# A hybrid DeltaNet/mLSTM layer on one core: masks of later heads moved along the projections, a fourth place for the scan's scaled values, sign changes as three-operand instructions

## The chip, the cores and the metric

The kernel runs on one core of one Trainium2 chip. The metric is the device time of one execution in microseconds (us), as the median of several runs. The engines are named as in the profile: PE (TensorE, matmuls; PEld are its weight loads), DVE (VectorE), ACT (ScalarE), POOL (GpSimd) and SP (SyncE, which here only issues DMAs).

## The reference, cut to what matters

One layer over 512 latent tokens with a prefix of 256 context tokens, all in float32, D_MODEL 1024. Two token mixers read one input projection: a bidirectional gated DeltaNet with 8 heads (called GDN here) and a bidirectional mLSTM with 4 heads. Their outputs are merged by gates, projected, and a gated MLP with a 3x3 convolution follows.

```
    kb = k * beta[..., None]
    a_strict = jnp.einsum('bhnld,bhnsd->bhnls', kb, k) * decay
    rhs = jnp.concatenate([v * beta[..., None], kb * jnp.exp(gc)[..., None]], axis=-1)
    sol = lax.linalg.triangular_solve(a_strict, rhs, left_side=True, lower=True, unit_diagonal=True)
    u, w = sol[..., :dv], sol[..., dv:]
...
        attn = jnp.einsum('bhnld,bhnsd->bhnls', q, k) * decay
...
        v_new = u_n - jnp.einsum('bhld,bhde->bhle', w_n, s)
        s_next = s * gt_n[..., None, None] + jnp.einsum('bhld,bhle->bhde', kt_n, v_new)
        o = jnp.einsum('bhld,bhde->bhle', qd_n, s) + jnp.einsum('bhls,bhse->bhle', at_n, v_new)
```

`decay` is exp of a masked difference of cumulated log decays, one 128x128 tile per chunk of 128 tokens and direction in the kernel: six chunks (two of context, four latent) by two directions are 12 tiles per GDN head, and four latent chunks by two directions are 8 tiles per mLSTM head.

## The kernel before, in words

**Stages.** After loads, modulation and the first norm, `mixers` (L1212) runs the two mixers; the rest (branch projections and gates, output projection, second norm, MLP) follows and is not touched. In the mixers each GDN head goes through `gdn_prep` (L714), `inverses` (L819, 16x16 triangular inverses on POOL, through DRAM), `merges` (L855, 16 to 128 by matmuls), `gdn_scan` (L956) and `gdn_tail` (L1019); each mLSTM head through `ml_prep` (L1057), `ml_scan` (L1126) and `ml_tail` (L1169). The preparation of heads 0 and 1 comes first, with nothing else to run. Then there is one step per head, s = 0 to 11: the scan of head s is driven by `drive` (L1195), which between two pieces of the scan draws pieces of the preparation of a head two or three ahead (and of early gate projections, `gate_mm` L1308) and of side work: the tail of head s-1, the merges of head s+1, gates of the mLSTM, and `ada_late` (L286), in which POOL weighs blocks of the matrix w_ada and adds them up, and a small matmul (`ada_sum` L316, tile `pad`) sums over partitions.

**Order.** Every instruction stands in its engine's queue in the order that the framework's tile scheduler gives from its own simulation, with hints: `queue_after` says that one instruction comes behind another on its queue, and `follow` (L1190) does that for the current anchor of an engine (the scan's newest matmul, DVE or ACT instruction). An engine runs its queue strictly in that order.

**Preparation of a GDN head.** Projections of context and latent tokens (`pc_k`, `px_k`, `px_q`, `pc_v`, `px_v`, `px_z`) run in float32r halves (three matmuls L124, L125 for each of eight blocks). `conv_silu` (L646) takes each out of its PSUM bank with a short convolution (ACT L653, DVE L654, L655, ACT tanh L656, DVE L657). `decays` and `weights` (L699, L706) make the decay tiles `Eg`: a DMA brings a row to all partitions, the DVE adds a column and takes the minimum with a mask (L710, 12 instructions of 128x128), and ACT takes exp (L711). For head 0 and heads 3 to 7 the 12 masks are written right behind the context part of the k projection, for heads 1 and 2 behind the q projection. The scalars `sc` (four per chunk and direction, 128x6) are made by

```
            nc.vector.tensor_tensor(s[:, 0, :], rk2, self.colB[:, :, 2 + d, h], ALU.mult)
            nc.vector.tensor_scalar(s[:, 1, :], s[:, 0, :], -1.0, None, ALU.mult)
            nc.vector.tensor_tensor(s[:, 2, :], s[:, 0, :], self.colB[:, :, d, h], ALU.mult)
            nc.vector.tensor_scalar(s[:, 3, :], s[:, 2, :], -1.0, None, ALU.mult)
```

(L754 to L757). The products `pkk` (L770, k by k) are scaled by `sc` and `Eg` into `Bt` (which lies in the buffer `gx` for most heads; L773, 12 DVE instructions), which frees the PSUM banks that `pqk` (L778, k by q) takes next; `at` (L782) reads `pqk`. Then v is turned to token-major (`ps_tm_v`) and ACT scales it into `vt` (L799); q follows (`ps_tm_q`, L804).

**Scan step of a GDN head.** `p1` (L980) = k S; `X` (L984, DVE) from it; `p2` (L988) = T X; ACT makes two scaled copies of `p2` for each of two directions: `v3` (L996), which goes into the state by `p3` (L1000) and `S` (L1005, L1007, DVE), and `v2` (L1013), which goes into the output by `po` (L971). All of them have the tile name "v", with three places.

**mLSTM.** `ml_prep` makes its masks `Em` (8, at L710 too) in front of the two `mo` projections. In `ml_scan`, `mp` (L1151) is read by ACT into `mn` (L1155), `mpc` (L1143) updates the state, and ACT L1165 makes `mo`. In the last steps the gate projections' tanh (L1312) is an ACT instruction that reads PSUM into `x1`.

PSUM has eight banks: two for the scan, one for merges, one for `po`, two for preparation (`pkk`, `pqk`, `ps_tm_*`) and two for projections ("acc").

Of the kernel before, what the change touches and what calls it, by code (L numbers as in the profile page):

```python
# [9 lines left out]
F32 = mybir.dt.float32  # L10
F32R = mybir.dt.float32r
BF16 = mybir.dt.bfloat16
AF = mybir.ActivationFunctionType
# [53 lines left out]
class Kern:  # L67
# [218 lines left out]
    def ada_late(self):  # L286

        nc, eng = self.nc, self.nc.gpsimd

        def load(j):  # L290
            w = self.hold.tile([P, 4, P], F32, tag="aw", name=f"aw{j}", bufs=3)
            i, c0 = j % 2, 2048 + P * (j // 2)
            self.follow(nc.sync.dma_start(w, self.I["w_ada"][0][512 * i : 512 * i + 512, c0 : c0 + P].rearrange("(k p) c -> p k c", p=P)))
            return w

        w = load(0)
        for j in range(64):
            nxt = load(j + 1) if j < 63 else None
            g = eng.tensor_tensor(w, w, self.sc[:, 4 * (j % 2) : 4 * (j % 2) + 4, 0:1].broadcast_to([P, 4, P]), ALU.mult)  # L299
            self.follow(g)  # L300
            self.follow(g, "q")
            eng.tensor_tensor(w[:, 0:2, :], w[:, 0:2, :], w[:, 2:4, :], ALU.add)  # L302
            if j % 2 == 0:
                a = self.hold.tile([P, P], F32, tag="as", name=f"as{j}", bufs=6)
                eng.tensor_tensor(a, w[:, 0, :], w[:, 1, :], ALU.add)
            else:
                eng.tensor_tensor(w[:, 0, :], w[:, 0, :], w[:, 1, :], ALU.add)
                eng.tensor_tensor(a, a, w[:, 0, :], ALU.add)
                self.sums.append((j // 2, a))
            for _ in range(2):  # L310
                if self.pad is not None and len(self.sums) > 1:
                    self.ada_sum()
            w = nxt
            yield
# [383 lines left out]

    def decays(self, h):  # L699
        E = [self.decay_rows(d, h, list(range(NCH)), f"g{h}_{d}") for d in range(2)]  # L700
        for d in range(2):
            if not 0 < h < 3:
                self.weights(E[d], d, h, range(NCH))
        return E

    def weights(self, E, d, row, g):  # L706

        nc = self.nc
        for c in g:
            self.follow(nc.vector.scalar_tensor_tensor(E[:, c, :], E[:, c, :], self.colA[:, c, d, row : row + 1], self.mask[d], ALU.add, ALU.min), "v")  # L710
        nc.scalar.activation(E[:, g[0] : g[-1] + 1, :], E[:, g[0] : g[-1] + 1, :], AF.Exp)  # L711


    def gdn_prep(self, h):  # L714
# [5 lines left out]
        kT = hold.tile([P, NALL], F32, tag="kT", name=f"kT{h}", bufs=3)  # L720
        p = yield from self.acc(wk, f"k{h}", True)
        self.conv_silu(p, NCTX, 8 + h, kT[:, :NCTX], {"v": self.chain["u"]} if h == 0 else None)
        E = self.decays(h)
        wq = self.w_cols(w, P * h, f"wq{h}") if h else self.first["wq"]
        p = yield from self.acc(wk, f"k{h}", False)
        self.conv_silu(p, NT, 8 + h, kT[:, NCTX:], {"v": self.chain["u"]} if h == 0 else None)
        wv = self.w_cols(w, 2048 + P * h, f"wv{h}") if h else self.first["wv"]
        qT = hold.tile([P, NT], F32, tag="qT", name=f"qT{h}", bufs=3)
        p = yield from self.acc(wq, f"q{h}", False)
        self.conv_silu(p, NT, h, qT, self.chain if h == 0 else None)  # L730
        if 0 < h < 3:
            v, self.anchor["v"] = self.anchor.get("v"), self.last_v
            for d in range(2):
                self.weights(E[d], d, h, range(NCH))
            self.anchor["v"] = v

        kt = hold.tile([P, NCH, P], F32, tag="kt", name=f"kt{h}", bufs=3)
# [14 lines left out]
        for d in range(2):  # L752
            s = hold.tile([P, 4, NCH], F32, tag=f"sc{d}", name=f"sc{h}_{d}", bufs=3)
            nc.vector.tensor_tensor(s[:, 0, :], rk2, self.colB[:, :, 2 + d, h], ALU.mult)  # L754
            nc.vector.tensor_scalar(s[:, 1, :], s[:, 0, :], -1.0, None, ALU.mult)
            nc.vector.tensor_tensor(s[:, 2, :], s[:, 0, :], self.colB[:, :, d, h], ALU.mult)
            nc.vector.tensor_scalar(s[:, 3, :], s[:, 2, :], -1.0, None, ALU.mult)  # L757
            sc.append(s)

        i = (h + 1) % 3  # L760
# [195 lines left out]
    def gdn_scan(self, h):  # L956
# [16 lines left out]
        for st in range(NCH):  # L973
# [18 lines left out]
            if st < NCH - 1:  # L992
                v3 = []
                for d, c in enumerate(cs):
                    v3.append(tmp.tile([P, P], F32, tag="v", name=f"v3_{h}", bufs=3))
                    self.anchor["s"] = nc.scalar.activation(v3[d], p2[:, d, :], AF.Copy, scale=sc[d][:, 2 + j, c : c + 1])  # L996
                yield
                p3 = self.pt([P, 2, P], "sc", f"p3_{h}")
# [10 lines left out]
            if cs[0] >= CC:  # L1009
                for d, c in enumerate(cs):  # L1010
                    x = c - CC
                    v2 = tmp.tile([P, P], F32, tag="v", name=f"v2_{h}", bufs=3)
                    nc.scalar.activation(v2, p2[:, d, :], AF.Copy, scale=sc[d][:, j, c : c + 1])  # L1013
                    out(x, qs[d][:, x * P : x * P + P], S[d])
                    out(x, at[d][:, x, :], v2)
# [41 lines left out]
    def ml_prep(self, h):  # L1057
# [12 lines left out]
        qT = hold.tile([P, NT], F32, tag="qT", name=f"mqT{h}", bufs=3)  # L1070
        p = yield from self.acc(wq, f"mq{h}", False)
        nc.scalar.activation(qT, p, AF.Copy, scale=P ** -0.5)
        for d in range(2):
            self.weights(E[d], d, 8 + h, range(CC, NCH))
        og = []
        for b in range(2):
            p = yield from self.acc(wo, f"mo{h}", False)
            if b == 0:
                wo = self.w_cols(w, O_MO + MDV * h + P, f"mwo{h}_1")
            g = hold.tile([P, NT], F32, tag=("zs", "vt")[b], name=f"og{h}_{b}", bufs=3)  # L1080
# [227 lines left out]
    def gate_mm(self, i, n, out):  # L1308

        wg = self.w_cols(self.I["w_in"][0], (O_G1, O_G2)[i] + P * n, f"wg{i}_{n}")  # L1310
        p = yield from self.acc(wg, f"g{i}_{n}", False)
        self.nc.scalar.activation(out, p, AF.Tanh, scale=0.5)  # L1312
        return out

    def merge(self):
# [302 lines left out]
```

## Time and profile before

| | us |
|---|---|
| median of 3 runs | 1338.4 (1337.61 to 1341.63) |
| profiled execution, its own time | 1334.85 |
| its span | 1333.1 |
| PE busy | 1290.1 (97%) |
| DVE busy | 898.9 (67%) |
| ACT busy | 584.3 (44%) |
| POOL busy | 532.1 (40%) |

The profile's page gives busy time by engine, the span in 40 slices, the chain of work that ended last, and groups of instructions by line. The trace behind it answers what each engine waited for, one line's instructions, busy time of stretches, and the instructions of an engine in order of time. The page's share of the chain that ended last is PE 71%, DVE 8%, ACT 5%. The profiled execution is one more execution beside the three runs; it lies 3.55 us under their median.

### The profile page before, as it was taken

How to read it: one execution, taken by the hardware profiler on the slowest of the kernel's cores; microseconds unless marked ns; L12 is line 12 of the kernel's file. 1: busy time of each engine (PE TensorE's matmuls, PEld its weight loads, DVE VectorE, ACT ScalarE, POOL GpSimd, SP SyncE). 2: the span in 40 equal slices, each digit the busy share in tenths (PEclk: the TensorE clock that was granted, in tenths of full speed). 3: DMA queues.
4: the chain of work that ended last, by engine and by line, in shares of the span. 5: the costliest groups of instructions: out<-in, count | busy, mean ns of one | idle time of the engine just before them, and what ended most of it. 6: DMA issues, size and time to landing. Idle time of an engine off the chain costs nothing.

```text
span 1333.1 us, 24202 instructions
## 1 busy us (share of the span) xinstructions
PE 1290.1 (97%) x9454; PEld 1093.3 (82%) x9454; DVE 898.9 (67%) x1809; ACT 584.3 (44%) x1283; POOL 532.1 (40%) x679
## 2 busy tenths in 40 slices
PE   6997999999999999999999999999999999999997
PEld 5887778888888888989888878888788888888886
DVE  6877777957868665343737476445669789997943
ACT  5565564555655644333334345222343333333322
POOL 4312330123121238575857560000444555554543
PEclk9999999999999999999999999999999999999999
DMA  9534233332242335254443433436333333333221
GB/s 284 151 106 123 45 86 98 72 87 73 61 108 60 74 84 143 78 160 111 125 121 104 112 100 88 127 111 227 104 111 95 95 95 96 95 98 90 81 102 73
DMA packets 233248, 141.86 MB, mean 106 GB/s; under 512 B 32992, under 2 KB 215533, under 8 KB 233133
## 3 DMA queue, kind: packets, MB, share of 16 engines
q1 hardware_dynamic: 230973, 140.09, 37.4%
q8 instruction: 74, 1.21, 0.4%
q10 hardware_dynamic: 2160, 0.23, 0.1%
q14 instruction: 41, 0.34, 0.1%
HBM read 134.47 MB, written 5.82 MB: 105 GB/s over the span
## 4 chain that ended last, share of the span: by engine, by line
PE 71%; DVE 8%; ACT 5%; DMA 2%; issue 1%; POOL 1%; SPq 0%; POOLq 0%; ACTq 0%; DVEq 0%
PE pu L124 12%; PE pd L124 6%; PE pu L125 6%; PE py L124 4%; PE px_g L124 4%; PE pv L124 3%; PE pd L125 3%; PE py L125 2%; PE px_mo L124 2%; PE px_g L125 2%; PE po L971 2%; PE p L988 2%; PE pv L125 2%; PE px_z L124 1%; PE p L980 1%
## 5 line engine op out<-in xcount | busy, mean ns | idle before, releaser
L1588 DVE SCALAR_TENSOR_TENSOR y<-pu,fw,y 128x441 f32<-128x441 f32 (+2 forms) x352 | 229.6, 690 | 38.7 <-ACT y L1579 33.0
L299 POOL TENSOR_TENSOR aw<-aw,sc 128x512 f32<-128x512 f32 x64 | 69.7, 1092 | 51.9 <-DMA aw<-in_w_ada_dram 51.9
L148 POOL TENSOR_TENSOR rs<-pw_t,mhalf 128x1 f32<-128x1 f32 x14 | 7.9, 563 | 161.1 <-PE po L125 130.4
L148 POOL TENSOR_TENSOR kh<-pw_t,phalf 128x6 f32<-128x6 f32 x8 | 10.9, 1361 | 127.9 <-DVE pw_t L147 36.0
L302 POOL TENSOR_TENSOR aw<-aw 128x256 f32<-128x256 f32 x64 | 56.1, 880 | 2.9
L842 POOL MEMSET gx<- 96x16 f32 x8 | 1.0, 124 | 119.1 <-DMA gx<-scr 119.1
L1517 POOL TENSOR_TENSOR al<-y,ah 128x512 fp32r<-128x512 f32 x22 | 28.6, 1300 | 31.2 <-ACT ah L1516 31.2
L1342 DVE SCALAR_TENSOR_TENSOR x<-x,py 128x512 f32<-128x512 f32 x16 | 11.0, 688 | 41.9 <-PE py L125 41.9
L1147 DVE SCALAR_TENSOR_TENSOR C<-C,ge,mpc 128x257 f32<-128x257 f32 x32 | 15.3, 478 | 34.9 <-PE mpc L1143 34.8
L656 ACT ACTIVATE cv_t<-cv_y 128x512 f32<-128x512 f32 (+1 forms) x40 | 22.0, 549 | 38.1 <-DVE cv_y L655 36.7
L847 POOL TENSOR_TENSOR iv_t<-gx 96x14 f32<-96x14 f32 (+6 forms) x112 | 35.1, 313 | 8.0
L849 POOL TENSOR_TENSOR gx<-gx,iv_t 96x14 f32<-96x14 f32 (+6 forms) x112 | 33.7, 301 | 8.7
L1579 ACT ACTIVATE y<-pu,fw 128x512 f32<-128x512 f32 x44 | 29.9, 683 | 13.3 <-PE pu L125 10.4
L996 ACT ACTIVATE v<-p,sc 128x128 f32<-128x128 f32 x80 | 25.2, 365 | 21.6 <-PE p L988 21.5
L984 DVE SCALAR_TENSOR_TENSOR X<-p,colA,vt 128x128 f32<-128x128 f32 x80 | 24.0, 339 | 15.5 <-PE p L980 15.1
L1516 ACT CAST ah<-y 128x512 fp32r<-128x512 f32 x22 | 13.6, 619 | 46.7 <-DVE y L1515 46.7
L1515 DVE TENSOR_TENSOR y<-y,y 128x512 f32<-128x512 f32 x22 | 31.3, 1424 | 0.9
L710 DVE SCALAR_TENSOR_TENSOR Eg<-Eg,colA,mask 128x128 f32<-128x128 f32 x96 | 27.4, 356 | 3.3 <-DMA Eg<-gd 3.3
L1155 ACT ACTIVATE mn<-mp,colA 128x257 f32<-128x257 f32 x32 | 15.2, 474 | 32.5 <-PE mp L1151 30.6
L971 PE MATMUL po<-v,at 128*128 128x128 f32 x128 | 26.0, 285 | 2.1 <-ACT v L1013 2.1
L1013 ACT ACTIVATE v<-p,sc 128x128 f32<-128x128 f32 x64 | 22.9, 375 | 11.7 <-PE p L1000 8.8
L1007 DVE SCALAR_TENSOR_TENSOR S<-S,ge,p 128x128 f32<-128x128 f32 x64 | 19.1, 338 | 12.4 <-PE p L1000 12.1
(1222 smaller groups left out, 4571.4 us busy)
## 6 DMA issues: line engine op xcount, KB each, us to landing
aw<-in_w_ada_dram SPq DMA_DIRECT2D x64, 256.0 KB
uw<-in_w_ada_dram SPq DMA_DIRECT2D x16, 512.0 KB
Eg<-gd SPq DMA_DIRECT2D x16, 384.0 KB
qs<-gd SPq DMA_DIRECT2D x16, 256.0 KB
xn<-in_x_dram SPq DMA_DIRECT2D x4, 512.0 KB
Em<-r1d SPq DMA_DIRECT2D x8, 256.0 KB
mwo_0r<-in_w_in_dram SPq DMA_DIRECT2D x4, 512.0 KB
mwo_1r<-in_w_in_dram SPq DMA_DIRECT2D x4, 512.0 KB
```

The source lines that it names most:

```text
L124: for i in (mm(out, lh, rh, start=start, stop=False), mm(out, lh, rl, start=False, stop=False), mm(out, ll, rh, start=False, stop=stop)):
L125: mm(out, ll, rh, start=False, stop=stop)):
L299: g = eng.tensor_tensor(w, w, self.sc[:, 4 * (j % 2) : 4 * (j % 2) + 4, 0:1].broadcast_to([P, 4, P]), ALU.mult)
L302: eng.tensor_tensor(w[:, 0:2, :], w[:, 0:2, :], w[:, 2:4, :], ALU.add)
L710: self.follow(nc.vector.scalar_tensor_tensor(E[:, c, :], E[:, c, :], self.colA[:, c, d, row : row + 1], self.mask[d], ALU.add, ALU.min), "v")
L847: eng.tensor_tensor(t, Bi[:, 0:j, j : j + 1].broadcast_to([8 * NB, j, n]), Bi[:, j : j + 1, j + 1 :].broadcast_to([8 * NB, j, n]), ALU.mult)
L849: g = eng.tensor_tensor(Bi[:, 0:j, j + 1 :], Bi[:, 0:j, j + 1 :], t, ALU.add)
L971: nc.tensor.matmul(self.po[h][:, x, :], a, b, start=False, stop=self.left == 0)
L1515: nc.vector.tensor_tensor(ys[0], ys[0], ys[1], ALU.mult)
L1517: nc.gpsimd.tensor_tensor(al[:, j, :], ys[0], ah[:, j, :].bitcast(F32), ALU.subtract)
L1579: nc.scalar.activation(y, ps, AF.Copy, scale=tap(0, 0))
L1588: g = nc.vector.scalar_tensor_tensor(o, u3[:, r0 + dy : r1 + dy, c0 + dx : c1 + dx], tap(dy, dx), o, ALU.mult, ALU.add)
```

## The change

It does six things.

1. `weights` becomes a generator that gives one mask at a time. For heads 3 to 7 a new helper `along` draws one mask per step of a projection: seven beside the latent k projection, the other five (and the two exp) beside the q projection. Head 0 draws all at once where they were, heads 1 and 2 behind the q projection as before. For mLSTM heads the masks are drawn along the second `mo` projection instead of in front of the first.
2. The tile "v" has four places instead of three.
3. The two negated scalars are made by a three-operand instruction straight from the inputs of the positive ones (`rk2` by -1 by a column; `s0` by -1 by a column), so that `s1` no longer reads `s0` and `s3` no longer reads `s2`.
4. `ada_sum` is drawn only when more than two sums are ready (was one).
5. The tanh of a gate projection follows the scan's newest ACT instruction once the early gates go to `x1` (the last mLSTM steps).
6. The DMA scratch of POOL is halved, which makes room in SBUF.

The number of instructions on each engine stays (DVE: 32 TENSOR_SCALAR become SCALAR_TENSOR_TENSOR); below `decays` lines move down by 12 to 15.

```diff
@@ ada_late
             for _ in range(2):
-                if self.pad is not None and len(self.sums) > 1:
+                if self.pad is not None and len(self.sums) > 2:
                     self.ada_sum()
@@
     def decays(self, h):
         E = [self.decay_rows(d, h, list(range(NCH)), f"g{h}_{d}") for d in range(2)]
-        for d in range(2):
-            if not 0 < h < 3:
-                self.weights(E[d], d, h, range(NCH))
-        return E
+        return E, chain(*(self.weights(E[d], d, h, range(NCH)) for d in range(2)))
+
+    def along(self, gen, work):
+
+        while True:
+            try:
+                x = next(gen)
+            except StopIteration as e:
+                for _ in work:
+                    pass
+                return e.value
+            next(work, None)
+            yield x
 
     def weights(self, E, d, row, g):
...
         for c in g:
             self.follow(nc.vector.scalar_tensor_tensor(E[:, c, :], E[:, c, :], self.colA[:, c, d, row : row + 1], self.mask[d], ALU.add, ALU.min), "v")
+            if c != g[-1]:
+                yield
         nc.scalar.activation(E[:, g[0] : g[-1] + 1, :], E[:, g[0] : g[-1] + 1, :], AF.Exp)
+        yield
@@ gdn_prep
-        E = self.decays(h)
+        E, masks = self.decays(h)
+        if h == 0:
+            for _ in masks:
+                pass
         wq = self.w_cols(w, P * h, f"wq{h}") if h else self.first["wq"]
-        p = yield from self.acc(wk, f"k{h}", False)
+        p = yield from self.along(self.acc(wk, f"k{h}", False), islice(masks, 7 if h > 2 else 0))
...
-        p = yield from self.acc(wq, f"q{h}", False)
+        p = yield from self.along(self.acc(wq, f"q{h}", False), masks if h > 2 else iter(()))
...
         if 0 < h < 3:
             v, self.anchor["v"] = self.anchor.get("v"), self.last_v
-            for d in range(2):
-                self.weights(E[d], d, h, range(NCH))
+            for _ in masks:
+                pass
             self.anchor["v"] = v
...
-            nc.vector.tensor_scalar(s[:, 1, :], s[:, 0, :], -1.0, None, ALU.mult)
+            nc.vector.scalar_tensor_tensor(s[:, 1, :], rk2, -1.0, self.colB[:, :, 2 + d, h], ALU.mult, ALU.mult)
             nc.vector.tensor_tensor(s[:, 2, :], s[:, 0, :], self.colB[:, :, d, h], ALU.mult)
-            nc.vector.tensor_scalar(s[:, 3, :], s[:, 2, :], -1.0, None, ALU.mult)
+            nc.vector.scalar_tensor_tensor(s[:, 3, :], s[:, 0, :], -1.0, self.colB[:, :, d, h], ALU.mult, ALU.mult)
@@ gdn_scan
-                    v3.append(tmp.tile([P, P], F32, tag="v", name=f"v3_{h}", bufs=3))
+                    v3.append(tmp.tile([P, P], F32, tag="v", name=f"v3_{h}", bufs=4))
...
-                    v2 = tmp.tile([P, P], F32, tag="v", name=f"v2_{h}", bufs=3)
+                    v2 = tmp.tile([P, P], F32, tag="v", name=f"v2_{h}", bufs=4)
@@ ml_prep
-        for d in range(2):
-            self.weights(E[d], d, 8 + h, range(CC, NCH))
         og = []
+        masks = chain(*(self.weights(E[d], d, 8 + h, range(CC, NCH)) for d in range(2)))
         for b in range(2):
-            p = yield from self.acc(wo, f"mo{h}", False)
+            p = yield from self.along(self.acc(wo, f"mo{h}", False), masks if b else iter(()))
@@ gate_mm
-        self.nc.scalar.activation(out, p, AF.Tanh, scale=0.5)
+        g = self.nc.scalar.activation(out, p, AF.Tanh, scale=0.5)
+        if self.slots is not None:
+            self.follow(g, "s")
@@ kernel
-    nc = _bacc.Bacc("TRN2", target_bir_lowering=False, num_devices=1, dynamic_dma_scratch_size=2048)
+    nc = _bacc.Bacc("TRN2", target_bir_lowering=False, num_devices=1, dynamic_dma_scratch_size=1024)
```

Since the scheduler deals the order anew, rows move on all engines. Three places matter most for what follows. In the rows a number behind a name tells tiles of one name apart.

**DVE, scalars and `Bt` of head 2** (during the scan of head 0), before:

```order
L754 TENSOR_TENSOR sc2_0_2010<-rk22_2004,colB_923 128x6
L754 TENSOR_TENSOR sc2_1_2015<-rk22_2004,colB_923 128x6
...
L755 TENSOR_SCALAR sc2_0_2010<-sc2_0_2010 128x6
L756 TENSOR_TENSOR sc2_0_2010<-sc2_0_2010,colB_923 128x6
L755 TENSOR_SCALAR sc2_1_2015<-sc2_1_2015 128x6
L756 TENSOR_TENSOR sc2_1_2015<-sc2_1_2015,colB_923 128x6
...
L773 SCALAR_TENSOR_TENSOR gx_83<-pkk2_2020,sc2_0_2010,Eg2_0_1704 128x128 x2
L757 TENSOR_SCALAR sc2_0_2010<-sc2_0_2010 128x6
L773 SCALAR_TENSOR_TENSOR gx_83<-pkk2_2020,sc2_1_2015,Eg2_1_1706 128x128
L757 TENSOR_SCALAR sc2_1_2015<-sc2_1_2015 128x6
L773 SCALAR_TENSOR_TENSOR gx_83<-pkk2_2020,sc2_1_2015,Eg2_1_1706 128x128
```

and now:

```order
L769 TENSOR_TENSOR sc2_0_2010<-rk22_2004,colB_923 128x6
L770 SCALAR_TENSOR_TENSOR sc2_0_2010<-rk22_2004,colB_923 128x6
L769 TENSOR_TENSOR sc2_1_2015<-rk22_2004,colB_923 128x6
L770 SCALAR_TENSOR_TENSOR sc2_1_2015<-rk22_2004,colB_923 128x6
...
L771 TENSOR_TENSOR sc2_0_2010<-sc2_0_2010,colB_923 128x6
L772 SCALAR_TENSOR_TENSOR sc2_0_2010<-sc2_0_2010,colB_923 128x6
L788 SCALAR_TENSOR_TENSOR gx_83<-pkk2_2020,sc2_0_2010,Eg2_0_1704 128x128
L771 TENSOR_TENSOR sc2_1_2015<-sc2_1_2015,colB_923 128x6
L772 SCALAR_TENSOR_TENSOR sc2_1_2015<-sc2_1_2015,colB_923 128x6
L788 SCALAR_TENSOR_TENSOR gx_83<-pkk2_2020,sc2_0_2010,Eg2_0_1704 128x128
```

The four negated scalars are three-operand instructions, and two of them stand ahead of the copies of `oTg` and X.

**PE, end of the preparation of head 0** (transposes of v, q and of head 1's k, against the v projection of head 1's context), before:

```order
L778 MATMUL pqk0_1128<-qT0_971,kT0_938 128x128 x4
L124 MATMUL px_q1_1355<-hx1_76,wq1h_1312 128x512
L125 MATMUL px_q1_1355<-hx0_75,wq1l_1313 128x512
L684 MATMUL ps_tm_v0_1238<-ident_84,vT0_1137 128x128 x2
L124 MATMUL pc_v1_1542<-hc0_81,wv1h_1350 128x256
```

and now:

```order
L684 MATMUL ps_tm_v0_1238<-ident_84,vT0_1137 128x128 x2
L124 MATMUL px_q1_1355<-hx0_75,wq1h_1312 128x512
L124 MATMUL px_q1_1355<-hx1_76,wq1h_1312 128x512
L125 MATMUL px_q1_1355<-hx0_75,wq1l_1313 128x512
L684 MATMUL ps_tm_v0_1243<-ident_84,vT0_1137 128x128 x4
L819 MATMUL ps_tm_q0_1252<-ident_84,qT0_971 128x128 x4
L684 MATMUL ps_tm_k1_1403<-ident_84,kT1_1273 128x128 x2
L124 MATMUL pc_v1_1542<-hc0_81,wv1h_1350 128x256
```

The second part of v's transposes, those of q, and the first of head 1's k now stand ahead of `pc_v1`. In the same way the four `pqk1` and two of head 1's `ps_tm_v1` now stand ahead of the whole of `pc_k2`, and the 24 matmuls of `pc_k2` ahead of the other four `ps_tm_v1`.

**ACT, a scan step of head 2** beside head 4's preparation, before:

```order
L996 ACTIVATE v3_2_4195<-p2_2_4192,sc2_0_2010 128x128
L996 ACTIVATE v3_2_4197<-p2_2_4192,sc2_1_2015 128x128
L1013 ACTIVATE v2_2_4229<-p2_2_4192,sc2_0_2010 128x128
L653 ACTIVATE cv_y_4205<-pc_v4_4173,cw_855 128x256
L833 COPY cg4_4062<-Bt4_4022 32x192 x4
L1013 ACTIVATE v2_2_4233<-p2_2_4192,sc2_1_2015 128x128
```

and now:

```order
L1011 ACTIVATE v3_2_4195<-p2_2_4192,sc2_0_2010 128x128
L1011 ACTIVATE v3_2_4197<-p2_2_4192,sc2_1_2015 128x128
L1028 ACTIVATE v2_2_4229<-p2_2_4192,sc2_0_2010 128x128
L1028 ACTIVATE v2_2_4233<-p2_2_4192,sc2_1_2015 128x128
L653 ACTIVATE cv_y_4205<-pc_v4_4173,cw_855 128x256
L848 COPY cg4_4062<-Bt4_4022 32x192 x4
```

The second `v2` no longer stands behind the convolution's and the inverse's copies.

In the last mLSTM steps the tanh moves likewise on ACT: of head 3's scan, the third `mn` stood behind the cast of a weight, a tanh and two `mo`, and now stands ahead of the cast and the tanh. The two last sums of `ada_late` now come together, behind the last early gate projection; the masks of mLSTM heads 2 and 3 still stand in a row of eight.

## Rows read from the trace of the kernel before

**Rows 1.** Stretch, length, busy PE, PEld, DVE, ACT, POOL (instructions); granted clock, DMA

```profile
100.00:200.00 100.00, 87.94 (x1037) 73.41 (x1036) 75.11 (x190) 58.62 (x160) 34.68 (x95) 0.95 0.33 85
300.00:400.00 100.00, 98.92 (x1026) 86.46 (x1025) 73.43 (x196) 58.46 (x180) 27.06 (x66) 1.00 0.31 81
```

**Rows 2.** Waits of PE: line waited for; total us, times, longest

```profile
PE ps_tm_v L684 <- ACT vt L799: 4.2, 1, 4.2
PE pqk L778 <- DVE gx L773: 3.0, 2, 2.5
PE pad L318 <- POOL as L308: 2.6, 4, 1.1
PE pc_v L124 <- ACT cv_y L653: 2.2, 1, 2.2
PE po L971 <- ACT v L1013: 2.1, 4, 0.6
PE w0p L880 <- DVE y L875: 1.4, 1, 1.4
...
PE mp L1151 <- ACT mn L1155: 1.4, 2, 0.9
PE pv L124 <- ACT va L1113: 1.3, 1, 1.3
...
PE ps_gt L638 <- DVE gx L773: 0.7, 1, 0.7
```

**Rows 3.** Instructions of lines L755, L756, L757: duration ns min/median/max

```profile
L755 DVE TENSOR_SCALAR sc<-sc x16: 154/157/1302, 94.3 to 469.8; 128x6 f32<-128x6 f32 x16
...
L756 DVE TENSOR_TENSOR sc<-sc,colB x16: 150/155/163, 94.4 to 469.9; 128x6 f32<-128x6 f32 x16
...
L757 DVE TENSOR_SCALAR sc<-sc x16: 149/1070/1127, 95.1 to 471.8; 128x6 f32<-128x6 f32 x16
```

**Rows 4.** DVE in order of time, 163 to 169 us: start, us, instruction

```profile
163.69 1.30 DVE L755 TENSOR_SCALAR sc<-sc 128x6 f32<-128x6 f32 x1
164.91 0.15 DVE L756 TENSOR_TENSOR sc<-sc,colB 128x6 f32<-128x6 f32 x1
...
168.00 1.04 DVE L757 TENSOR_SCALAR sc<-sc 128x6 f32<-128x6 f32 x1
```

**Rows 5.** POOL in order of time, the same stretch

```profile
163.68 5.34 POOL L925 TENSOR_TENSOR qs<-qs,qT 128x512 f32<-128x512 f32 x4
```

**Rows 6.** PE in order of time, 100 to 140 us, with idle before and releaser

```profile
100.47 0.38 PE L684 MATMUL ps_tm_v<-ident,vT 128*128 128x128 f32 x2
...
130.32 0.93 PE L684 MATMUL ps_tm_v<-ident,vT 128*128 128x128 f32 x4 [4.19 <-ACT vt L799]
...
139.73 0.98 PE L880 MATMUL w0p<-gx,y 32*32 32x16 f32 x96 [1.41 <-DVE y L875]
```

**Rows 7.** DVE in order of time, 102 to 126 us

```profile
102.78 1.28 DVE L782 TENSOR_TENSOR at<-pqk,Eg 128x512 f32<-128x512 f32 x2
...
122.97 2.66 DVE L773 SCALAR_TENSOR_TENSOR Bt<-pkk,sc,Eg 128x128 f32<-128x128 f32 x10
```

**Rows 8.** Busy time by stretch, behind the wait of Rows 6

```profile
130.30:134.00 3.70, 3.68 (x13) 3.24 (x14) 0.85 (x3) 2.65 (x13) 0.00 (x0) 0.54 0.71 231
```

**Rows 9.** ACT in order of time, 311 to 314 us

```profile
311.63 1.43 ACT L833 COPY cg<-Bt 32x192 f32<-32x192 f32 x4 [2.99 <-DVE Bt L773]
313.09 0.37 ACT L1013 ACTIVATE v<-p,sc 128x128 f32<-128x128 f32 x1
```

**Rows 10.** DVE in order of time, 670 us

```profile
670.82 2.98 DVE L710 SCALAR_TENSOR_TENSOR Em<-Em,colA,mask 128x128 f32<-128x128 f32 x8 [6.38 <-DMA Em<-r1d]
```

**Rows 11.** PE in order of time, 789 to 792 us, with idle before and releaser

```profile
789.27 0.70 PE L1151 MATMUL mp<-C,mqT 128*128 128x257 f32 x2 [0.85 <-ACT mn L1155]
791.05 0.38 PE L318 MATMUL pad<-ones,as 128*128 128x2 f32 x2 [1.07 <-POOL as L308]
```

**Rows 12.** The page's groups of instructions, the masks: count, busy us, mean ns

```profile
L710 DVE SCALAR_TENSOR_TENSOR Eg<-Eg,colA,mask 128x128 f32<-128x128 f32 x96 | 27.4, 356 | 3.3 <-DMA Eg<-gd 3.3
```

## The prediction

> **What bounds the kernel now.** I read busy time by stretch first. PE is busy for 98.92 of 100 us in a typical stretch of the scans, and 87.94 of 100 between 100 and 200 us, where heads 0 and 1 are prepared and the first scan starts [rows 1]. So the kernel is bound by PE, and only time in which PE stands, or runs at the lower of its two clocks (1.2 and 2.4 GHz), can be won; the instruction counts stay, so PE's own work stays too. DVE is at 73.43 of 100 in the scans [rows 1]: it has room on average, and matters only through what PE waits for. Second I read what PE waits for. The waits that the edits can touch are 4.2 us for `vt`, 3.0 and 0.7 us for `Bt` (the `gx` of L773), 2.6 us in four waits for the sums of `ada_late`, 2.2 us for a convolution's first step, 2.1 us in four waits for `v2`, 1.4 us for the first merge's copy, 1.4 us for `mn` and 1.3 us for `va` [rows 2], 18.9 us together. Third I read the engines in order of time around the larger ones.
>
> **Sign changes.** The 16 tensor_scalar instructions of L757 work on 6 elements per partition, and yet their median is 1070 ns; one of L755 took 1302 ns. The two-input multiply of L756 on the same shape never took more than 163 ns [rows 3]. Around 165 us the order of time shows the pair: 1.30 us for L755, 0.15 us for the L756 right behind it, 1.04 us for an L757 [rows 4], all while POOL multiplies `qs` without a break from 163.68 for 5.34 us [rows 5]. So what is slow is one kind of instruction under POOL's load, not DVE as a whole. The three-operand form with two inputs does not occur on this shape with POOL at work; its cost lies between 0.15 us (as L756, nearest in shape and in its two tensor inputs) and 1.07 us (as L757). I take 0.15. In head 2 four instructions then give back about 3.7 us of DVE in front of the twelve `Bt`, more than the 2.5 us that `pqk` waits for them, so that wait goes; in head 3 the two waits of 0.5 and 0.7 us for `Bt` go in the same way. In later heads nothing waits for `Bt` in view: the projections that are drawn beside the scan cover it. Term: 3.7 us less [rows 2]; the other end is 0.
>
> This is where a rule speaks against the change. The Trainium skill (GPSIMD Engine Reference, section Key points) says that POOL shares its SBUF interfaces with DVE and contends with DVE instructions in a 2-port mode or with two SBUF inputs. By the second half of that rule the new instructions would be held as well, and the term would be 0 instead of 3.7; L756, with two SBUF inputs, at 0.15 us inside POOL's 5.34 us disagrees [rows 4, 5].
>
> **Heads 0 and 1: the new order of PE.** Nothing else is there to run, so waits stand open. `pc_v1` waits 2.2 us and the second part of `ps_tm_v1` 4.2 us [rows 2]; now other rows stand in front of them. They do not vanish, since what they are waiting for is DVE and ACT work, which is unchanged. At the first place PE comes to the transposes of q (`ps_tm_q0`), whose bank is free only when the two `at` of L782 are done, at 102.78 + 1.28 = 104.06 [rows 7]; PE is there at about 101.7 by my reckoning: the first transposes of v ended at 100.47 + 0.38 = 100.85 [rows 6], three matmuls of px_q1 only change places with them, and four more transposes follow. So it waits about 2.3 us there instead. At the second, the ten `Bt` of 2.66 us [rows 7] now stand ahead of the convolution that frees the bank of `pc_k2`, which therefore waits, about 2.3 us by my reckoning; then some 0.7 us remains at `ps_tm_v1`. So 6.4 us of waits become about 5.3: 1.1 us less. Beside it there is the clock. The stretch behind the wait of 4.2 us ran at 0.54 of full clock for 3.70 us [rows 8], which costs 3.70 x 0.46 = 1.7 us, and the same shows behind the wait of 2.2 us. If both new waits of 2.3 us bring such a spell too, 1.1 us is all; if neither does, 1.1 + 2 x 1.7 = 4.5. The wait of 1.4 us for the first merge [rows 6] stays, since its input is a chain through POOL that starts only some 1.5 us earlier. I take 1.7, nearer to the low end because the waits are long as before; ends 0 and 4.5.
>
> **Four places for v.** The second `v2` of a step needs the place that an earlier `v3` leaves when `p3` has read it, so the scheduler puts it late: behind four copies `cg` of 1.43 us, so that it starts at 313.09 [rows 9] while `po` is waiting for it. With four places all four scaled copies stand together in front of these. Four waits of about 0.5 us go: 2.1 us [rows 2]. What was behind them, the four `cg`, comes 0.37 us later, in a chain that has slack beside the scan. The other end is 0.
>
> **Sums, tanh.** With a third sum asked for, a `pad` comes later than POOL's result. Of the four waits (2.6 us, the longest 1.1 [rows 2]) I count the one at 791.05, 1.07 us [rows 11], and about 0.4 of the small ones. The one in the preparation of the last mLSTM head I count as nothing: DVE can start the masks of mLSTM head 3 only when their DMA has landed (670.82, after 6.38 us of idling [rows 10]), the `va` that PE then waits 1.3 us for stands behind their exp on ACT, and that DMA is issued behind PE's work in the same stretch, which the new order does not pull forward; what PE wins before it, it waits longer there. The masks of that head stay in a row of eight, so part 1 of the change does not reach it. The tanh that follows the scan lets `mn` go first: the wait at 789.27, 0.85 us [rows 11]. Term: 1.5 + 0.85 = 2.3 us; ends 0 and 5.3 (all three groups, 2.6 + 1.4 + 1.3).
>
> **Masks one per step.** The instructions stay the same: 96 in 27.4 us, 0.285 us each [rows 12]. In front of PE none is waited for before. Cost 0: what hides them is the projection whose steps they are drawn beside, and DVE's idle quarter. Where that cover is gone, each costs up to 0.285 us (first rival). The DMAs that bring the rows stay where they are in the program; SP's queue is not moved past anything. The smaller DMA scratch costs nothing: no transfer is issued by POOL.
>
> **Sum.** 3.7 + 1.7 + 2.1 + 2.3 = 9.8 us less. Against it I set 1 us of new small waits, since all rows are dealt anew and short waits lie in every scan: 8.8 less. The profiled execution took 1334.85 us, so 1326.05; its time is 3.55 us under the median of the runs shown, 1338.4, and the same distance gives **1329.6 us**.
>
> **Rivals.**
> *Slower by masks in the scan.* 76 masks (60 of heads 3 to 7 and 16 of mLSTM heads 0 and 1) now stand one by one among X, S and the copies of the merges, which PE reads next. For: DVE runs in strict order at 73 of 100, and a scan step is a chain through DVE. Against: PE has projections to fill in with, and single masks hold an X up by 0.285 us where a row of twelve held it by 3.4. The price is 0.285 each; all that wait would be 76 x 0.285 = 21.7 us. With more than 8.8 / 0.285 = 31 of them on PE's path the change loses; with 45 it is 4.0 us (0.3%) slower, with 60 it gives 1338.4 - 8.8 + 17.1 = 1346.7. Chance 0.09.
> *Given back.* The waits of heads 0 and 1 come back whole with their half-speed spells, the sums and tanh only let PE wait at the next exp or `mn`, and of the rest something like half is real: 0.5 x (3.7 + 2.1) less 1 = 1.9 us, 1336.5. For: heads 0 and 1 have no filler, and the 1.3 us wait for `va` is already a wait that takes what is won before it. Chance 0.18.
> *The signs do not do what they say.* If POOL holds the new instructions too, 3.7 falls away: 5.1 less, 1333.3. For: both inputs lie in SBUF like those of the slow ones. Against: L756. That is the rule of the Trainium skill named above (GPSIMD Engine Reference, Key points), and the trace so far stands against it. Chance 0.13.
>
> **The numbers.** 0.60 is left for the forecast. A measurement of this kernel can tell about 0.3%, 4.0 us, from no change. The forecast and most of the third rival (4.0 us is passed by 1.1) are faster: 0.60 + 0.11 = 0.71; the second rival and the remainder of the third are no change: 0.20; slower is the first rival: 0.09. For the range, all best ends together are 3.7 + 4.5 + 2.1 + 5.3 = 15.6 us, 1322.8, less a little for waits not counted: 1321.5. Upward it reaches over the second rival's 1336.5 to 1337.5. The first rival and the tails are left out.
>
> **What would show it.** Right: L770 and L772 at about 0.15 us also between 163 and 169 us, and no wait of `pqk` there; `po` waiting for L1028 nowhere; no wait of about 1 us at a `pad` or `mp` near 790; PE's busy share between 100 and 200 us higher by one to four points, with waits on `at` and a convolution in place of that on `vt`. Wrong: L770 and L772 near 1 us under POOL; a wait of PE for X, S or merge copies (L999, L1022, L922) that is new in 200 to 500 us, behind single L719; more half-speed spells than three before 145 us.

## The result and the profile after

The changed kernel takes 1321.67 us (median of 5 runs, 1318.97 to 1323.87) against 1338.4 us before; the ratio is 0.9873, with a 95% interval of 0.9854 to 0.9893. That is 17 us less, where the forecast had 8.8. The profiled execution took 1323.87 us, so between the two traces 11.0 us are to be found. This trace is of the slowest of the five runs, 2.2 us above their median, where the trace of before lies 3.55 us under its own.

The first part of the page, and busy time by stretch, of the changed kernel:

```profile
PE 1284.0 (97%) x9454; PEld 1089.1 (82%) x9454; DVE 888.1 (67%) x1809; ACT 585.0 (44%) x1283; POOL 531.3 (40%) x679
```

```profile
100.00:200.00 100.00, 88.23 (x1059) 72.61 (x1057) 75.50 (x192) 60.51 (x163) 34.07 (x95) 0.97 0.35 86
...
300.00:400.00 100.00, 99.94 (x1120) 86.54 (x1118) 71.72 (x199) 58.03 (x174) 27.02 (x66) 1.00 0.32 81
```

Against [rows 1], PE has one point more in the scans, and it started 1120 matmuls in those 100 us where it started 1026: the stretch holds other work, but a busy share that rises by one point cannot show how much was won. Between 100 and 200 us the share rose by 0.3 points, not by the one to four that the forecast named as a sign. The waits of PE in the changed kernel:

```profile
PE pv L124 <- ACT va L1127: 2.6, 1, 2.6
PE w0p L895 <- DVE y L890: 2.3, 1, 2.3
PE pc_k L124 <- DVE cv_y L655: 2.2, 1, 2.2
PE ps_tm_v L684 <- ACT vt L814: 1.9, 1, 1.9
PE y0p L888 <- DVE gx L882: 1.8, 1, 1.8
...
PE ps_tm_q L819 <- DVE at L797: 0.6, 1, 0.6
...
PE mp L1165 <- ACT mn L1169: 0.5, 1, 0.5
...
PE pqk L793 <- DVE gx L788: 0.4, 1, 0.4
```

Of [rows 2], the waits for `v2` and for the sums are gone, `pqk`'s fell from 3.0 to 0.4, `mp`'s from 1.4 to 0.5. The wait of 4.2 us for `vt` is gone from its old place; one of 1.9 us stands earlier, in the preparation of head 0 (it ends at 102.66). New are `pc_k`, `y0p` and `ps_tm_q`; `w0p` and `va` grew. Where the two traces part shows best at marks that both have (start of the first matmul in us; the last column is of the unrounded starts):

| mark on PE | before | after | ahead by |
|---|---|---|---|
| k projection of head 2 | 131.7 | 129.5 | 2.2 |
| first merge's w0p | 139.7 | 139.4 | 0.4 |
| z projection of head 2 | 170.7 | 168.1 | 2.6 |
| k projection of head 4 | 283.4 | 279.2 | 4.2 |
| k projection of mLSTM head 0 | 503.7 | 491.3 | 12.4 |
| k projection of mLSTM head 3 | 684.9 | 674.4 | 10.5 |
| last early gate projection | 806.9 | 793.6 | 13.2 |
| first up projection of the MLP | 954.8 | 941.9 | 12.9 |
| end of the span | 1333.1 | 1322.2 | 10.9 |

Most is won between the k projection of head 4 and that of mLSTM head 0: 8.2 us, in a stretch in which the waits of before amount to 2.1.

### The profile page after: what moved, and what is told of

Read it like the earlier page. It is cut to its first block, busy times and chain, and to the rows that moved or that the text cites. A ratio compares the mean times of both kernels' runs of the same rounds, so it can differ in the third digit from the quotient of the medians.

```text
span 1322.2 us, 24197 instructions
## 1 busy us (share of the span) xinstructions
PE 1284.0 (97%) x9454; PEld 1089.1 (82%) x9454; DVE 888.1 (67%) x1809; ACT 585.0 (44%) x1283; POOL 531.3 (40%) x679
## 4 chain that ended last, share of the span: by engine, by line
PE 77%; DVE 6%; ACT 2%; DMA 2%; issue 1%; SPq 0%; POOL 0%; POOLq 0%; ACTq 0%; DVEq 0%
PE pu L124 12%; PE pd L124 6%; PE pu L125 6%; PE py L124 4%; PE px_g L124 4%; PE pv L124 3%; PE pd L125 3%; PE py L125 2%; PE px_g L125 2%; PE px_mo L124 2%; PE po L986 2%; PE pv L125 2%; PE p L1003 2%; PE px_q L124 1%; PE px_z L124 1%; PE px_v L124 1%
## 5 line engine op out<-in xcount | busy, mean ns | idle before, releaser
L148 POOL TENSOR_TENSOR rs<-pw_t,mhalf 128x1 f32<-128x1 f32 x14 | 7.9, 563 | 161.8 <-DVE pw_t L147 160.1
L148 POOL TENSOR_TENSOR kh<-pw_t,phalf 128x6 f32<-128x6 f32 x8 | 11.2, 1395 | 129.4 <-DVE pw_t L147 129.4
L302 POOL TENSOR_TENSOR aw<-aw 128x256 f32<-128x256 f32 x64 | 52.4, 822 | 2.9
L1011 ACT ACTIVATE v<-p,sc 128x128 f32<-128x128 f32 x80 | 25.5, 368 | 37.7 <-PE p L1003 37.5
L1531 DVE TENSOR_TENSOR y<-y,y 128x512 f32<-128x512 f32 x22 | 27.9, 1266 | 0.9
L995 PE MATMUL p<-S,kT 128*128 128x128 f32 x160 | 27.7, 281 | 0.7 <-DVE S L1022 0.5
L1045 POOL TENSOR_TENSOR fo<-fo,mhalf 128x4 f32<-128x4 f32 x8 | 8.5, 1069 | 48.5 <-DVE fo L1044 48.5
```

Of the source, the lines that this page charges most:

```text
L995: g = nc.tensor.matmul(p1[:, d, :], kT[:, c * P : c * P + P], S[d], start=True, stop=True)
L1531: nc.vector.tensor_tensor(ys[0], ys[0], ys[1], ALU.mult)
```

## The experiments

"Before" ran beside them 23, 17 and 11 times, with medians of 1337.28, 1337.22 and 1336.56. Ratios are against it. What a kernel takes less than before is worked out from the ratio; what it takes more or less than the changed kernel is the difference of the two medians. The changed kernel was timed at another time, when before took 1338.4, so such a difference of two or three us is not clear of noise; where it matters the traces are compared at the same place.

**Each part alone, on the kernel before.**

```diff
-                    v3.append(tmp.tile([P, P], F32, tag="v", name=f"v3_{h}", bufs=3))
+                    v3.append(tmp.tile([P, P], F32, tag="v", name=f"v3_{h}", bufs=4))
...
-                    v2 = tmp.tile([P, P], F32, tag="v", name=f"v2_{h}", bufs=3)
+                    v2 = tmp.tile([P, P], F32, tag="v", name=f"v2_{h}", bufs=4)
```

> The kernel before with four places for v (and the smaller scratch that makes room) and nothing else. Theory A (the forecast's term: only the visible waits of po for v2 go): 2.1 us less, 1336.3 against 1338.4. Theory B (with four scaled copies ready at once the matmuls of a scan step also stand together on PE, and the short gaps at each change between scan, merge and projection matmuls go as well; the trace of the changed kernel is some 8 us ahead over heads 4 to 7): 6 to 8 us less, about 1331.

1330.06 us, ratio 0.994 (0.9925 to 0.9954): 8.0 us less (6.2 to 10.0). Theory B.

```diff
-            nc.vector.tensor_scalar(s[:, 1, :], s[:, 0, :], -1.0, None, ALU.mult)
+            nc.vector.scalar_tensor_tensor(s[:, 1, :], rk2, -1.0, self.colB[:, :, 2 + d, h], ALU.mult, ALU.mult)
...
-            nc.vector.tensor_scalar(s[:, 3, :], s[:, 2, :], -1.0, None, ALU.mult)
+            nc.vector.scalar_tensor_tensor(s[:, 3, :], s[:, 0, :], -1.0, self.colB[:, :, d, h], ALU.mult, ALU.mult)
```

> The kernel before with the three-operand sign changes and nothing else. Theory A (forecast): 3.7 + 1.7 = 5.4 us less, about 1333. Theory B (from the trace of the changed kernel: the lead of 2.3 us that the preparation of heads 0 and 1 wins is given back at the first merge, whose two waits are 1.8 and 2.3 us there; what stays is the wait of pqk in head 2 and those of head 3): 2.5 to 3.7 us less, about 1335. L755 and L757 at 0.15 to 0.2 us under POOL's load in both.

1330.2 us, ratio 0.995 (0.9938 to 0.9963): 6.7 us less, above both theories, nearer to A. The last sentence of the expectation failed: four of the new instructions took 1.27 us.

For the masks, `decays`, `along`, `weights` and the loops of `gdn_prep` and `ml_prep` as in the change, nothing else:

> The kernel before with masks one per step and nothing else. Theory A (forecast): no change, 1338.4 within 2 us. Theory B (masks that no longer stand twelve in a row let X, S and copies of the merges through earlier, and part of the lead in heads 4 to 7 comes from that): 3 to 5 us less. Rival: masks stand in front of the scan, up to 8 us more.

1334.6 us, ratio 0.9978 (0.9964 to 0.9991): 2.9 us less (1.2 to 4.8). That is more than nothing and nearer to theory B, but it does not rule out theory A's 2 us.

```diff
-                if self.pad is not None and len(self.sums) > 1:
+                if self.pad is not None and len(self.sums) > 2:
...
+        if self.slots is not None:
+            self.follow(g, "s")
```

> The kernel before with sums drawn when three are ready and the tanh behind the scan's ACT instruction, nothing else. Theory A (forecast): 2.3 us less, about 1336. Theory B (the trace of the changed kernel gains 2.8 us around the last gate projections but loses 1.7 us with a wait of 2.6 us for va and a half-speed spell around 660): 1.1 us less, about 1337.

1336.31 us, ratio 0.9987 (0.9974 to 0.9999): 1.7 us less (0.1 to 3.5), between the two, which it cannot tell apart. PE's wait for `va` was 2.7 us in its trace, as in that of the whole change.

**The change without one part.** These undo the same lines in the changed kernel.

> The changed kernel with three places for v again (and the larger scratch). If the parts add up: 8.0 us more than the changed kernel, about 1329.7. If the signs and the masks already take away the waits of po (2.1 us) and what is left of this part is fewer changes between merge matmuls and 128x128 matmuls on PE (80 in heads 4 to 7 here against 64 in the changed kernel and 96 before): about 4 us more, 1325.5.

1323.98 us, ratio 0.9891 (0.9867 to 0.9915): 2.3 us more than the changed kernel, not clear of noise, and far from the 8.0 that this part is worth alone. The parts don't add up: signs and masks had taken away the waits of `po` already. What is left shows in the stretch of heads 4 to 7, which is 2.9 us longer (table below).

> The changed kernel with the masks in rows of twelve and eight as before. If the forecast's cost of 0 for the masks holds: 1321.7 within 1.5. If the masks alone (2.9 us less than before) act by the order of PE, 80 changes between kinds in heads 4 to 7 here against 64: 2 to 3.5 us more, about 1324.5.

1322.24 us, ratio 0.9871 (0.9848 to 0.9893): 0.6 us more, no difference. On the whole time the forecast's 0 holds, though the stretch of heads 4 to 7 is 2.0 us longer (table below); its trace has one spell of 3.4 us less at the lower of PE's two clocks (1.7 us), which hides that. Such half-speed spells come back below.

> The changed kernel with the four scalars made as before. If the parts add up (signs alone 6.7 us): 1328.4. If the other parts already take away half of it (the order of heads 0 and 1 is the old one here, so at least the 2.3 us there and the 2.5 us of pqk come back): 1326 to 1327. L755 and L757's slow instructions come back under POOL's load in both.

1326.46 us, ratio 0.9914 (0.9896 to 0.9933): 4.8 us more, as the second account expected. The slow instructions are back (four of them, up to 1.30 us), and `pqk`'s wait of 2.5 us.

**What PE loses without waiting.** In the stretch from head 4's k projection to mLSTM head 0's, I counted in every trace how often PE goes from a merge's small matmul (32 or 64 rows) to a larger one or back:

| kernel | stretch, us | changes | PE's waits, us |
|---|---|---|---|
| before | 220.3 | 96 | 2.1 |
| signs alone | 217.8 | 96 | 0 |
| masks alone | 215.5 | 80 | 0 |
| four places alone | 214.5 | 80 | 0 |
| all but four places | 215.0 | 80 | 0 |
| all but masks | 214.1 | 80 | 0 |
| the change | 212.1 | 64 | 0.1 |
| all but signs | 212.1 | 64 | 0.1 |

The waits are worth 2.5 us (first two rows), and each 16 changes fewer 2 to 3.7. Before, `po` was split by the missing place:

```profile
312.02 0.39 PE L971 MATMUL po<-v,at 128*128 128x128 f32 x2
312.24 0.39 PE L971 MATMUL po<-S,qs 128*128 128x128 f32 x2
312.56 0.43 PE L913 MATMUL wp<-gx,y 32*32 32x32 f32 x14
313.51 0.49 PE L971 MATMUL po<-v,at 128*128 128x128 f32 x2 [0.52 <-ACT v L1013]
```

With four places alone, the same 38 small matmuls of the merge (14 and 24 above) run in one piece behind the last `po`:

```profile
313.02 0.39 PE L971 MATMUL po<-v,at 128*128 128x128 f32 x2
313.33 0.72 PE L913 MATMUL wp<-gx,y 32*32 32x32 f32 x38
```

To price a change by itself, two kernels add the same 42 matmuls to the changed kernel, and differ only in their place in PE's queue:

```diff
+        z = None
+        n_ = 0
...
+                    n_ += 1
+                    self.queue_after(g, z)
+                    if h > 0 and n_ % 4 == 0:
+                        for _ in range(1):
+                            z_ = nc.tensor.matmul(wx[:, NCH:, :], self.ident, self.ident, start=True, stop=True)
+                            self.queue_after(z_, g if z is None or _ == 0 else z)
+                            z = z_
```

(together: `n_ == 24` and `range(6)`; `wx` is the merge's bank with 128 columns more.)

> The changed kernel with six added 128x128 float32 matmuls per merge of heads 1 to 7 (42 in all, identity by identity into unused columns of the merge's bank, nothing of the result changes), one behind every four of the 24 small matmuls wp. Against the next kernel it has 32 more excursions between small and 128x128 matmuls on PE (214 changes against 150) and the same instructions. Theory B (each excursion costs PE about 0.2 us that no wait shows): 5 to 7 us more than the next kernel. Theory A (PE loses only where it waits): the same as the next kernel within 1.5 us.

> The same 42 added matmuls, the six of a merge together behind its 24 small ones. In both theories their own work, 42 x 0.22 = 9.3 us, on top of the changed kernel's 1321.7, less what of it fills open waits: 1329 to 1331.

Apart 1338.88 us (ratio 1.001, 0.9996 to 1.0024), together 1330.09 us (0.9933, 0.9909 to 0.9957): 8.8 us between the medians and 10.3 by the ratios for 64 changes more, 0.14 to 0.16 us each. Theory A is out, and theory B's 5 to 7 us was too low. "Together" came where both had it. PE in order of time, apart:

```profile
310.43 0.31 PE L931 MATMUL wp<-gx,y 32*32 32x32 f32 x8
310.67 0.49 PE L936 MATMUL wp<-ident 128*128 128x128 f32 x2
311.09 0.31 PE L931 MATMUL wp<-gx,y 32*32 32x32 f32 x8
311.33 0.49 PE L936 MATMUL wp<-ident 128*128 128x128 f32 x2
```

and together:

```profile
307.81 0.85 PE L931 MATMUL wp<-gx,y 32*32 32x32 f32 x48
308.59 1.60 PE L936 MATMUL wp<-ident 128*128 128x128 f32 x12
309.95 0.47 PE L125 MATMUL px_v<-hx,wv4l 128*128 128x512 f32 x1
```

Four small matmuls (x8: two instructions each) and one added one take 0.66 us from start to start when alternating, 6 x 0.66 = 4.0 for a merge; together the same 30 take 309.95 - 307.81 = 2.14. Where it goes shows in the starts: the two instructions of one added matmul hold the next small one up by 311.09 - 310.67 = 0.42 us, while twelve of them in a row take 309.95 - 308.59 = 1.36, 0.11 each. The added matmuls write to the bank of the small ones, but that is not the reason: in the traces of before, of the changed kernel and of these two a small matmul starts 0.2 us behind a large one of 128x128 (median 0.205), whether that is an added one or a `po` or `p` of the scan, which write to other banks (above, two `po` at 312.24 and the next small one at 312.56). No row of either has an idle time, and PE counts as busy in both. This is what the views of waits and of busy time can't show.

**Once more the kernel before.**

> The kernel before once more, for a second trace: its executions range over 8 us, and the trace that the forecast was made from lies 2.4 us under the median of the runs since. If that difference lies in the parts the change touches, a slower execution shows longer waits (for va behind the DMA of the last masks near 670 us, 1.3 us in the first trace against 1.6 to 2.7 in most others) and one more half-speed spell; if it lies elsewhere (first loads, second norm) the change's parts are the same in both.

1338.83 us, span 1337.1, 4.0 more than the first trace. The waits are mostly as before (3.0 for `pqk`, 1.2 for `va`), and two are shorter (3.4 for `vt`, 1.4 for the sums). What makes it longer is the granted clock: 23.9 us at the lower level before the last stretch, against 10.2. The same three stretches, in the first trace:

```profile
129.00:136.00 7.00, 5.68 (x22) 4.87 (x23) 2.08 (x6) 3.96 (x17) 0.00 (x0) 0.76 0.58 178
...
170.00:173.50 3.50, 3.50 (x21) 3.02 (x20) 3.50 (x12) 0.00 (x0) 0.00 (x0) 1.00 0.01 3
958.50:965.50 7.00, 7.00 (x61) 7.00 (x60) 3.52 (x6) 1.31 (x4) 3.12 (x3) 1.00 0.00 0
```

and in the second:

```profile
129.00:136.00 7.00, 5.24 (x17) 4.50 (x18) 3.23 (x8) 4.00 (x17) 0.00 (x0) 0.51 0.62 187
...
170.00:173.50 3.50, 3.01 (x13) 3.01 (x14) 3.50 (x13) 0.47 (x1) 0.15 (x1) 0.51 0.00 0
958.50:965.50 7.00, 6.16 (x30) 6.19 (x31) 4.19 (x7) 1.74 (x3) 4.32 (x4) 0.51 0.00 0
```

So the second half of my expectation holds, and half of the first: the slow stretch at 170 us begins at the end of `pqk`'s wait (2.5 us, up to 170.49), which the change takes away. In the first trace the same wait of 2.5 us ended at 169.35 and no slow stretch followed.

**What gives the lead of heads 0 and 1 back.** The new order put one DMA of head 2's decay rows between the store of head 0's inverses and their load. SP's queue and ACT's first use, before:

```profile
124.29 0.32 SPq L851 DMA_DIRECT2D scx<-gx  x1
125.97 0.37 SPq L852 DMA_DIRECT2D cdx<-scx  x1
...
127.99 0.93 SPq L692 DMA_DIRECT2D Eg<-gd  x2
```

```profile
128.95 0.80 ACT L866 ACTIVATE gx<-cdx,pm 128x192 f32<-128x192 f32 x2 [1.67 <-DMA cdx<-scx]
```

and after:

```profile
124.42 0.32 SPq L866 DMA_DIRECT2D scx<-gx  x1
125.15 0.32 SPq L692 DMA_DIRECT2D Eg<-gd  x1
127.34 0.37 SPq L867 DMA_DIRECT2D cdx<-scx  x1
```

```profile
133.55 0.80 ACT L881 ACTIVATE gx<-cdx,pm 128x192 f32<-128x192 f32 x2 [4.79 <-DMA cdx<-scx]
```

The load takes 6.2 us instead of 3.0, and y0p waits for it. The edit:

```diff
-        nc.sync.dma_start(cx, scx.rearrange("c b j i -> (b j) c i"))
+        self.bx.append(nc.sync.dma_start(cx, scx.rearrange("c b j i -> (b j) c i")))
...
+            if row == 2:
+                self.queue_after(g, self.bx[0])
```

> The changed kernel with one thing more: the two DMAs that bring the decay rows of head 2 (384 KB each) are issued behind the load of head 0's inverses (cdx), one of which the new order put ahead of it. In the changed kernel that load is issued at 127.34 and lands at 133.55, 6.2 us, against 125.97 and 128.95, 3.0 us, in the kernel before. If that is what gives the lead of heads 0 and 1 back: the wait of y0p (1.8 us) goes, the wait of w0p falls from 2.3 to about 1.4, the half-speed spell of 6.8 us shrinks to 3.4 (1.7 us): 3 to 4.5 us less than the changed kernel, about 1318. If the load is late for its own sake: no change, 1321.7 within 1.5.

1317.16 us, ratio 0.9856 (0.9839 to 0.9873): 4.5 us less than the changed kernel between the medians (2.3 by the ratios), by the first account. In the traces it is 0.4 us ahead of the changed kernel at head 2's k projection and 3.5 at head 2's z projection, and still 3.5 at mLSTM head 0: 3.1 us are won in this place. ACT's row is now

```profile
129.69 0.80 ACT L883 ACTIVATE gx<-cdx,pm 128x192 f32<-128x192 f32 x2 [1.71 <-DMA cdx<-scx]
```

y0p doesn't wait, `w0p` waits 1.4, and the spell behind them is 3.4 us long.

**The exp ahead of `va`.**

```diff
+                if VA[i] == 0:
+                    self.lastva = g
...
-        nc.scalar.activation(E[:, g[0] : g[-1] + 1, :], E[:, g[0] : g[-1] + 1, :], AF.Exp)
+        x = nc.scalar.activation(E[:, g[0] : g[-1] + 1, :], E[:, g[0] : g[-1] + 1, :], AF.Exp)
+        if row > 8:
+            self.queue_after(x, self.lastva)
```

> The kernel before this one with the exp of an mLSTM head's masks behind the last copy va of the head before on ACT. If the wait of PE for va (2.6 us, with a half-speed spell of 3.4 us that costs 1.7) is the exp's doing: 3 to 4 us less than the kernel before this one, about 1314.5. If the masks are then late for mp (L1108) instead: no less.

1314.6 us, ratio 0.9834 (0.9817 to 0.985): 2.6 us less again, a little under the expectation. PE waits for `va` nowhere, and nothing waits for the later exp. This version beats both kernels: 22 us less than before.

## Why the prediction was right or wrong

**The direction was right, the size half.** The step that failed first is the one on what bounds the kernel: "only time in which PE stands, or runs at the lower of its two clocks, can be won". PE also loses at every change between small and larger matmuls, in rows that count as busy (0.14 to 0.16 us each), and the new order has fewer of them: 64 for 96 in heads 4 to 7.

By place, the 11.0 us between the traces are 0.4 up to the first merge (for 1.7), 3.8 in heads 2 and 3 (for 3.7), 8.2 in heads 4 to 7 (for 2.1) and 0.8 from there to the last early gate projection (for 2.3), less 2.3 lost behind it (for the 1 us set against), where the change touches nothing (a wait of 1.6 us that was 0.9, and a spell of 3.4 us at 945.6). The measured 1321.67 lies just inside the range, whose end was all four terms at their best; it came there by another way, so that is luck.

**Four places.** The term was 2.1 us, the four waits. Alone it is worth 8.0 (6.2 to 10.0); in the stretch of heads 4 to 7 of its trace 5.8: 2.5 for the waits, the rest for 16 changes fewer. The mechanism was right, but the term stopped at the waits.

**Signs: right number, wrong reason.** The waits of the term of 3.7 fell to 0.4, and heads 2 and 3 gave 2.2 + 1.6 = 3.8 us (table of marks). That the number fits is in part luck: in the trace of the signs alone head 2 gave 2.4 and head 3 only 0.3 (a wait of 1.3 us for X is new there), and heads 4 to 7 gave 2.5, which the term did not have. Alone the edit is worth 6.7. As for the reason, I took L756 at 0.15 us inside POOL's 5.34 [rows 4, 5] as proof that instructions with two SBUF inputs are not held, against the rule of the Trainium skill (GPSIMD Engine Reference, section Key points). The changed kernel's DVE and POOL around head 2 show them held:

```profile
163.31 1.28 DVE L771 TENSOR_TENSOR sc<-sc,colB 128x6 f32<-128x6 f32 x1
164.52 0.15 DVE L772 SCALAR_TENSOR_TENSOR sc<-sc,colB 128x6 f32<-128x6 f32 x1
164.60 0.34 DVE L788 SCALAR_TENSOR_TENSOR gx<-pkk,sc,Eg 128x128 f32<-128x128 f32 x1
164.86 1.00 DVE L771 TENSOR_TENSOR sc<-sc,colB 128x6 f32<-128x6 f32 x1
165.78 0.16 DVE L772 SCALAR_TENSOR_TENSOR sc<-sc,colB 128x6 f32<-128x6 f32 x1
```

```profile
163.15 3.95 POOL L940 TENSOR_TENSOR qs<-qs,qT 128x512 f32<-128x512 f32 x3
```

(The three multiplies end at 164.57, 165.84 and 167.09.)

A small instruction that starts while POOL runs one of its multiplies ends when that multiply ends; the next one, if it follows at once, slips in before POOL's next. L756 of [rows 4] had run in such a gap. So the trace agrees with the second half of the rule after all: L771 has two SBUF inputs. That L755 and L757 of before, with one tensor input, were held as well has its reason in no row. What the edit wins is order: the eight small instructions now stand together. In head 2 two are held instead of four (both L771, so that the forecast's sign, L770 and L772 at about 0.15 us, came true by their places in the order and not by their form), and from head 3 on none, since all eight are through before the multiply of `qs` starts:

```profile
246.25 0.16 DVE L771 TENSOR_TENSOR sc<-sc,colB 128x6 f32<-128x6 f32 x1
...
246.49 0.16 DVE L772 SCALAR_TENSOR_TENSOR sc<-sc,colB 128x6 f32<-128x6 f32 x1
```

```profile
245.99 1.36 POOL L148 TENSOR_TENSOR kh<-pw_t,phalf 128x6 f32<-128x6 f32 x1 [26.76 <-DVE pw_t L147]
247.33 2.50 POOL L940 TENSOR_TENSOR qs<-qs,qT 128x512 f32<-128x512 f32 x2
```

With the signs alone, the last L757 of heads 4 to 7 still falls into the multiply, in the new form:

```profile
305.75 0.15 DVE L756 TENSOR_TENSOR sc<-sc,colB 128x6 f32<-128x6 f32 x1
305.82 1.27 DVE L757 SCALAR_TENSOR_TENSOR sc<-sc,colB 128x6 f32<-128x6 f32 x1
```

The third rival had the rule right and its consequence wrong.

**Heads 0 and 1.** I took 1.7 us; 2.2 was won up to head 2's k projection and 0.4 was left at the first merge. The new waits came where I put them (`pc_k` 2.2 against my 2.3; at q's transposes 0.6, and 1.9 for `vt` just in front of them, against 2.3). What failed is the wait of 1.4 us at the first merge, which I took to stay: it became 1.8 and 2.3, with a spell of 6.8 us behind. Behind that lies the sentence that SP's queue is not moved past anything: I followed PE, DVE and ACT through the new order and not SP, where a DMA went ahead of the inverses' load. Undone, it is worth 3.1 us in the traces.

**Sums and tanh.** 2.3 forecast, 1.7 (0.1 to 3.5) alone. As forecast, what this part wins ahead of the exp of the last masks PE waits there: in its own trace PE came to `va` 1.6 us earlier and was let go 0.2 earlier. But the forecast that the new order does not pull the masks' DMA forward was wrong: in the changed kernel it is issued at 652.5 for 664.7, so that of the lead only 1.3 us went into this wait (2.6 for 1.3). Not forecast was that this wait too is followed by a half-speed spell in the changed kernel (662.3 us, 3.4 us long).

**Masks.** 0 forecast, 2.9 less alone, nothing on top of the rest. The rival in which they hold up the scan didn't happen: no wait of PE for X or S in the scans of the changed kernel is longer than 0.5 us.

**From trace to median.** I took the profiled execution's distance to the median, 3.55 us, as fixed. Between the traces the sum was 2.2 us short (8.8 for 11.0); between the medians 7.9. The other 5.7 come from this step: the trace of before lay 3.55 under its median and that of the changed kernel 2.2 above its own. The first trace of before was a quick one: its second has 13.7 us more at the lower clock and is 4.0 us longer, with waits that are mostly the same. So a wait costs its length and, in some executions, a spell behind it, and a trace with few spells makes the waits look cheap.

## What to carry to other kernels

When small and large matmuls interleave on PE, count the changes between them in the queue before and after an edit: here each cost about 0.15 us that no view of waits or busy time shows. Follow a new order through the DMA queue too: one transfer of 384 KB between a store and the load of the same data cost 3.1 us in the traces. Before taking a term from one trace, take a second one, and look where the granted clock differs.

## What the runs showed of the hardware

That DVE's small instructions wait for the end of POOL's running multiply (0.7 to 1.3 us for six elements) and go at 0.15 us at its boundaries, whichever form they have, was not expected; nor that they run undisturbed beside POOL's 1.36 us L148 on six elements. The clock's half-speed spells came in lengths of 3.4 or 6.8 us, and with mostly the same waits in the same kernel one execution had 10.2 us of them before the last stretch and another 23.9.
